# A hybrid attention and RWKV-7 layer: substitution of both token halves on 128 partitions, the correction systems as a second line of work, decay on the summed state, aligned tiles, other rates

## The chip, the core and the metric

The kernel runs on one core of a Trainium2 chip. The metric is device time in microseconds (us) of one execution; three executions were timed, and one more was profiled. In the profile PE is the matrix engine (PEld its weight loads), DVE the vector engine, ACT the scalar engine, POOL the GpSimd engine, SP the engine that issues most DMAs. SBUF is the on-chip memory of 128 partitions, PSUM the matmul's accumulators. L540 is line 540 of the kernel.

## What is computed

One layer over 1024 tokens of width 1024, in float32. Half of the width is eight attention heads, the other half eight heads of a recurrence that runs over the tokens in both directions.

```python
h = _rms_norm(x, ln1_g[layer])
proj = h @ w_in[layer]                       # 1024 x 3328
q, k, v = ...; u = proj[..., 3 * ATTN_WIDTH:]
attn = _dilated_window_attention(q, k, v, q_norm_g[layer], k_norm_g[layer])
rwkv = _rwkv7_bidirectional(u, ...)
x = x + jnp.concatenate([attn, rwkv], axis=-1) @ w_out[layer]
h = _rms_norm(x, ln2_g[layer])
x = x + jnp.square(jax.nn.relu(h @ w_up[layer])) @ w_down[layer]

# the recurrence, per head and direction, state is 64 x 64
def step(state, inp):
    r_t, w_t, k_t, v_t, kk_t, a_t = inp
    s_kk = jnp.einsum('bhvk,bhk->bhv', state, kk_t)
    state = (state * w_t[:, :, None, :]
             - s_kk[..., None] * (kk_t * a_t)[:, :, None, :]
             + v_t[..., None] * k_t[:, :, None, :])
    return state, jnp.einsum('bhvk,bhk->bhv', state, r_t)
```

Attention is a mixture of three dilated windows with normed queries and keys.

## The kernel before

**Matmuls.** Values and weights of the large products are split into a high and a low part (`split_w`, L101 on ACT and L102 on DVE), and `mm3` (L104 to L107) adds three products of 128x512. There are 1248 of them in the input projection, 384 in the output projection, 3072 in the MLP.

**Projection.** `dense` is a generator that makes one tile of 128 columns after the other, in the fixed list `order`, and yields after every six matmuls; a tile is 48 matmuls. Tiles of the recurrence are mixed with their neighbour tokens and stay in SBUF; q, k and v tiles are normed (`qk_tile`, the small PE products `psq`) or transposed and written to DRAM.

**Preparation of the recurrence.** The tokens are cut into 16 chunks of 64. For each of four head pairs p, two token halves hf (8 chunks each) and two directions d, `unit_a` makes what a chunk needs: decayed keys and values in `al` and `bk`, their products G (PE `psg` L501, masked by DVE L506), and the transposed keys `BK` (PE `psb` L517). Before the transposes POOL multiplies the keys by the chunk's whole decay into `bks` (L512). Most of it goes to the DRAM records `rec_dr`. Then 64x64 triangular systems are solved. Their 16x16 diagonal blocks are taken through DRAM (`gd`) into `MP`, 64 partitions holding the 64 blocks of 8 chunks and 2 heads, and are inverted by forward substitution: 15 steps, each a product on DVE (`stmp`, L540) and a sum (L542) into `Tt`, which two POOL memsets start. The result goes through the DRAM scratch `td` into `t16` and `t16t`. `unit_c` then completes the inverse by four groups of 16 small products (PE `psd`, L560), each followed by one DVE operation (L566, L572, L575). All tiles of a unit have one buffer, but for G, kt, t16t and Yt with two.

**Order of the work.** `merge` interleaves two yields of one unit's `unit_a` with one of the `unit_c` before it; `drive` runs that and gives `dense` 0.35 yields after each. What is left of the projection runs between the steps of the recurrence. The program is written in this order with priorities (`ahead`), and a scheduler then sets the order on each engine, which is fixed: an instruction that waits holds up what is behind it on its engine, and on SP every DMA behind it.

**Recurrence.** `mixers` runs 16 steps, in each one chunk forward and one backward (`step`). A step is three dependent groups of eight products in `psc` (L846, L854, L859) with copies between them. The state of the next chunk is the third group plus the old state times the chunk's decay LC; POOL makes that product (`pl`, L852), DVE adds (L861). `fill(20, 6)` puts 20 yields of projection, or once that is done 6 pieces of attention, behind each step. There are 64 pieces of attention, 8 for each head, and the ends of the four head pairs.

**Tail.** `tail` does the output projection with what is left of attention, the second norm and the MLP in four groups of an up phase and a down phase of 384 matmuls each.

The scheduling calls before the change are these:

```python
drive(per_half(w), rate)
for d in range(2):
    prev = drive(merge(unit_a(p * 4 + hf * 2 + d, w, d), prev), rate)
```

Of the kernel before, what the change touches and what calls it, by code (L numbers as in the profile page):

```python
# [16 lines left out]
P = 128  # L17
# [30 lines left out]
def tile_trunk(ctx: ExitStack, tc: tile.TileContext, xT, w_in, w_o, w_up, w_dn, vecs, w2w0, a2, g2, cst, att,  # L48
# [102 lines left out]
    qg8 = cp.tile([P, 1], F32, name="qg8")  # L151
    nc.vector.tensor_scalar(qg8, V("qg"), HD ** -0.5, None, ALU.mult)
# [9 lines left out]
    def in_proj():  # L162
        with ExitStack() as st:
# [36 lines left out]
            with tc.tile_pool(name="xp", bufs=2, side="right", reuse_waits="tile") as xp:  # L200
# [49 lines left out]
                rstd = hp.tile([P, 8], F32, name="rstd")  # L250
# [115 lines left out]

            def until(c):
# [15 lines left out]

            def merge(a, prev):
                c = unit_c(prev) if prev is not None else iter(())
                pat = 'aac'
                i = 0
                v = None
                while a is not None or c is not None:
                    which = pat[i % len(pat)] if i < 100 else 'a'  # L390
                    i += 1
                    if (which == 'a' or c is None) and a is not None:
                        try:
                            next(a)
                        except StopIteration as e:
                            v = e.value
                            a = None
                    else:
                        if next(c, 1) == 1:
                            c = None  # L400
                    yield
                return v
# [49 lines left out]
            def unit_a(u, w, d):  # L452
# [57 lines left out]
                bks = up.tile([P, 8, 2, 64], F32, name="bks")  # L510
                for h in range(2):
                    nc.gpsimd.tensor_mul(bks[H[h]], bk[H[h], :, h:h + 2],  # L512
                                         lc[H[h]].rearrange("p (c o x) -> p c o x", o=1, x=1).to_broadcast([64, 8, 2, 64]))
                pss = [pg.tile([P, 8, 64], F32, name="psb", tag="psg") for h in range(2)]
                for c in range(8):
                    for h in range(2):
                        nc.tensor.transpose(pss[h][:, c], bks[H[h], c].rearrange("p a b -> p (a b)"), K("id2")[H[h]])  # L517
                yield
                BK = up.tile([P, 8, 2, 64], F32, name="BK", tag="bks")
# [3 lines left out]
                MP = up.tile([64, 16, 16], F32, name="MP")  # L523
                nc.sync.dma_start(MP, diag(gd))
                Ab = up.tile([P, 8, 64], F32, name="Ab")
                for h in range(2):
                    nc.sync.dma_start(Ab[H[h]], mats(gd, h))
# [4 lines left out]
                Tt = up.tile([64, 16, 16], F32, name="Tt")  # L532
                Tp = up.tile([64, 16, 16], F32, name="Tp")
                nc.gpsimd.memset(Tt, 0.0)
                nc.gpsimd.memset(Tt.rearrange("p a b -> p (a b)")[:, 0:256:17], 1.0)  # L535
                for s in range(1, 16):
                    t = s if d == 0 else 15 - s
                    rs = slice(0, s) if d == 0 else slice(16 - s, 16)
                    tmp = up.tile([64, 16, 16], F32, name="stmp")
                    nc.vector.tensor_mul(tmp[:, 0:s, 0:s], Tt[:, rs, rs],  # L540
                                         MP[:, rs, t:t + 1].rearrange("p a o -> p o a").to_broadcast([64, s, s]))
                    nc.vector.tensor_reduce(Tt[:, rs, t], tmp[:, 0:s, 0:s], axis=AX.X, op=ALU.add)  # L542
                nc.vector.tensor_copy(Tp, Tt.rearrange("p a b -> p b a"))
                t16 = up.tile([P, 8, 64], F32, name="t16")
                t16t = up.tile([P, 8, 64], F32, name="t16t", bufs=2)
                for src, dst, td in ((Tp, t16, tdr[u % 2]), (Tt, t16t, tdr[2 + u % 2])):
                    nc.sync.dma_start(diag(td), src)
                    for h in range(2):
                        nc.sync.dma_start(dst[H[h]], mats(td, h))
                return dict(p=p, d=d, cs=cs, Ab=Ab, t16=t16, t16t=t16t)  # L550
# [47 lines left out]
            prev = None  # L598
            for p in range(4):
# [18 lines left out]
                rate = (0.35,0.35,0.35,0.35,0.35)[p]  # L618
                for hf in range(2):
                    w = dict(p=p, hf=hf, kr=kr, rr=rr, vr=vr, wh=wh, wl=wl, kt=[])  # L620
                    drive(per_half(w), rate)
                    for d in range(2):
                        prev = drive(merge(unit_a(p * 4 + hf * 2 + d, w, d), prev), rate)
                        if d == 1:
                            drive(bonus(w), rate)
            drive(unit_c(prev), (0.35,0.35,0.35,0.35,0.35)[4])
# [188 lines left out]
    def mixers(st, st2, filler, T, tqs, pq_):  # L815
# [24 lines left out]
        def step(d, s, w, wn, psY):  # L840
# [8 lines left out]
            if wn is not None:  # L849
                pl = rt.tile([P, 4, 64], F32, name=f"pl{d}")  # L850
                for h in range(2):
                    nc.gpsimd.tensor_mul(pl[H[h]], pv[H[h], :, H[h]], LC[H[h], d, c].rearrange("p (r o) -> p r o", o=1).to_broadcast([64, 4, 64]))  # L852
# [4 lines left out]
            if wn is not None:  # L857
                for r, h in RH:
                    nc.tensor.matmul(ps[H[h], 0, r], rec[:, r, 256 + h * 64:320 + h * 64], uv[:, r, H[h]], start=True, stop=True)  # L859
                for h in range(2):  # L860
                    nc.vector.tensor_add(wn["pv"][H[h], :, H[h]], ps[H[h], 0], pl[H[h]])  # L861
# [312 lines left out]
```

## Time and profile before

| | us |
|---|---|
| median of the timed executions | 1860.64 |
| lowest and highest of the three | 1854.66, 1874.15 |
| the profiled execution | 1866.15 |
| its span, first to last instruction | 1864.4 |
| mean granted clock of PE | 0.922 |

A row of a table of stretches gives, after the stretch and its length, the busy time of each engine with its number of instructions, the granted clock of PE as a share of full speed, the mean busy share of the 16 DMA engines, and GB/s. Overlapping matmuls count once. A row of a group gives line, engine, operation, written tile, read tiles, shape and count, then busy time and mean ns of one, then the idle time just before them and what ended it. A row of a source line gives the shortest, median and longest duration in ns. A row of the timeline gives start, duration, instruction and count. A row of waits gives who waited for whom, us in total, times, longest us.

### The profile page before, as it was taken

To read this page: it belongs to the slowest core of one execution; us is meant where nothing else is said; L and a number is where in the kernel's file an instruction comes from. 1 tells how busy PE (TensorE), PEld (TensorE's weight loads), DVE (VectorE), ACT (ScalarE), POOL (GpSimd) and SP (SyncE) were. 2 spreads that over 40 slices of the span, in tenths; PEclk is the share of its full clock that TensorE was granted. 3 is DMA by queue.
4 is the path that set the end of the run, shared out by engine and by line. 5 is a ranking of instruction groups with operands and counts; after the bars stand their busy time and mean duration, and the time that the engine had idled before them with its cause. 6 is when DMAs were issued, how large, how long until landed. Compare 5 with 4: busy or idle time off the path is not lost.

```text
span 1864.4 us, 30214 instructions
## 1 busy us (share of the span) xinstructions
PE 1718.9 (92%) x11912; PEld 1401.8 (75%) x11912; DVE 919.7 (49%) x1941; ACT 547.0 (29%) x994; POOL 365.5 (20%) x409
## 2 busy tenths in 40 slices
PE   7999988899866999899899869999999999999999
PEld 6776767677655788688788757888888888888887
DVE  6677868787864344256554437432233233223321
ACT  5533323443310232255452415211121112112210
POOL 3043234352340111112110015210121012001200
PEclk9998978788865999889879889999999999999999
DMA  6157675688785986999683211111111111111121
GB/s 201 36 130 163 146 150 119 143 181 188 151 165 122 291 255 183 195 238 264 186 237 78 78 44 57 45 46 51 51 46 46 46 50 47 51 46 46 46 91 57
DMA packets 336285, 222.06 MB, mean 119 GB/s; under 512 B 237936, under 2 KB 289024, under 8 KB 332048
## 3 DMA queue, kind: packets, MB, share of 16 engines
q1 hardware_dynamic: 305520, 195.82, 40.5%
q10 hardware_dynamic: 27040, 14.31, 2.8%
q0 software_dynamic: 3584, 10.00, 2.5%
q8 instruction: 94, 1.54, 0.4%
q14 instruction: 47, 0.39, 0.1%
HBM read 150.22 MB, written 69.84 MB: 118 GB/s over the span
## 4 chain that ended last, share of the span: by engine, by line
PE 47%; issue 1%; DMA 1%; DVE 1%; POOL 1%; ACT 1%; SPq 0%; ACTq 0%; DVEq 0%; POOLq 0%
PE ps L105 14%; PE ps L106 14%; PE ps L107 14%; PE pvb L729 1%; PE ps_s L684 1%; PE ps_s L685 1%; PE ps_pt L723 1%; PE pv L711 0%; PE pv L710 0%; PE ps_pt L702 0%; PE ps_t L798 0%; DMA w3raw<-in_w_o 0%; POOL sq L1026 0%; POOL on L794 0%; DVE y L886 0%
## 5 line engine op out<-in xcount | busy, mean ns | idle before, releaser
L101 ACT CAST w3h<-w3raw 128x512 fp32r<-128x512 f32 (+1 forms) x152 | 90.9, 598 | 391.3 <-PE ps L106 386.8
L106 PE MATMUL ps<-h2l,w3h 128*128 128x512 f32 x512 | 202.6, 396 | 0.6 <-DVE h2l L1019 0.6
L105 PE MATMUL ps<-h2h,w3h 128*128 128x512 f32 x512 | 202.4, 396 | 0.7 <-DVE x L997 0.7
L107 PE MATMUL ps<-h2h,w3l 128*128 128x512 f32 x512 | 202.5, 395 | 0.0
L1063 POOL TENSOR_TENSOR relu<-relu 128x512 f32<-128x512 f32 x64 | 76.7, 1200 | 543.1 <-DVE relu L1062 543.1
L105 PE MATMUL ps_u<-hh,wh 128*128 128x512 f32 x368 | 156.1, 424 | 2.8 <-DVE ur L305 2.3
L107 PE MATMUL ps_u<-hh,wl 128*128 128x512 f32 x368 | 155.1, 421 | 0.0
L106 PE MATMUL ps_u<-hl,wh 128*128 128x512 f32 x368 | 155.0, 421 | 0.0
L102 DVE TENSOR_TENSOR w3l<-w3raw,w3h 128x512 fp32r<-128x512 f32 (+1 forms) x152 | 106.7, 702 | 79.2 <-ACT w3h L101 79.1
L1071 DVE TENSOR_TENSOR x<-x,ps 128x512 f32<-128x512 f32 x64 | 44.0, 688 | 187.6 <-PE ps L107 187.6
L540 DVE TENSOR_TENSOR stmp<-Tt,MP 64x1 f32<-64x1 f32 (+14 forms) x240 | 105.4, 439 | 47.8 <-POOL Tt L535 28.7
L105 PE MATMUL ps<-f,w3h 128*128 128x512 f32 x320 | 126.6, 397 | 0.6 <-ACT f L806 0.6
L106 PE MATMUL ps<-rw,w3h 128*128 128x512 f32 x320 | 126.8, 396 | 0.0
L105 PE MATMUL ps<-rw,w3h 128*128 128x512 f32 x320 | 126.7, 397 | 0.0
L107 PE MATMUL ps<-rw,w3l 128*128 128x512 f32 x320 | 126.6, 396 | 0.0
L106 PE MATMUL ps<-f,w3h 128*128 128x512 f32 x320 | 126.6, 396 | 0.0
L107 PE MATMUL ps<-f,w3l 128*128 128x512 f32 x320 | 125.2, 392 | 0.0
L105 PEld LDWEIGHTS ps<-h2h,w3h 128*128 128x128 f32 x512 | 96.2, 188 | 24.6 <-ACT w3h L101 1.1
L106 PEld LDWEIGHTS ps<-h2l,w3h 128*128 128x128 f32 x512 | 96.2, 188 | 24.5 <-DVE h2l L1019 1.1
L107 PEld LDWEIGHTS ps<-h2h,w3l 128*128 128x128 f32 x512 | 96.3, 188 | 23.7
L1062 DVE SCALAR_TENSOR_TENSOR relu<-ps,rep 128x512 f32<-128x512 f32 x64 | 44.1, 691 | 116.4 <-PE ps L107 116.2
L105 PEld LDWEIGHTS ps_u<-hh,wh 128*128 128x128 f32 x368 | 73.5, 200 | 21.6 <-DVE ur L305 2.9
(324 smaller groups left out, 3410.7 us busy)
## 6 DMA issues: line engine op xcount, KB each, us to landing
rec<-rec_dr SPq DMA_DIRECT2D x32, 1152.0 KB, 8.9
w3raw<-in_w_up SPq DMA_DIRECT2D x64, 256.0 KB, 2.7
w3raw<-in_w_dn SPq DMA_DIRECT2D x64, 256.0 KB, 2.7
raw<-in_w_in SPq DMA_DIRECT2D x46, 256.0 KB, 3.2
rec_dr<-al POOLq DMA_DIRECT2D x64, 128.0 KB, 3.9
rec_dr<-G SPq DMA_DIRECT2D x32, 256.0 KB, 4.6
rec_dr<-G SPq DMA_DIRECT2D x64, 128.0 KB, 3.7
rec_dr<-BK ACTq DMA_DIRECT2D x16, 512.0 KB, 4.8
```

Source lines behind the costliest of these rows:

```text
L101: nc.scalar.copy(hi, raw)
L102: nc.vector.tensor_sub(lo, raw, r2f(hi))
L105: nc.tensor.matmul(ps, lh, rh, start=start, stop=False)
L106: nc.tensor.matmul(ps, lh, rl, start=False, stop=False)
L107: nc.tensor.matmul(ps, ll, rh, start=False, stop=stop)
L540: nc.vector.tensor_mul(tmp[:, 0:s, 0:s], Tt[:, rs, rs], MP[:, rs, t:t + 1].rearrange("p a o -> p o a").to_broadcast([64, s, s]))
L684: nc.tensor.matmul(ps[:, i], qh[:, qs], kk[:, ks], start=True, stop=False)
L685: nc.tensor.matmul(ps[:, i], ql[:, qs], kk[:, ks], start=False, stop=True)
L723: nc.tensor.transpose(pt[:, x, i * P:(i + 1) * P], sb[:, i, x * P:(x + 1) * P], ident)
L1062: nc.vector.scalar_tensor_tensor(t, pss[hf], 0.0, rep[:, HS[hf]], ALU.max, ALU.mult)
L1063: nc.gpsimd.tensor_mul(t, t, t)
L1071: nc.vector.tensor_add(x1[c][:, HS[hf]], x1[c][:, HS[hf]], ps)
```

## The change

1. `unit_a` ends with the writes to DRAM. A new generator `pair_b` takes both token halves of a head pair and direction: the half hf lies on its 64 partitions of `MP`, `Tt`, `Tp` and `stmp`, so 120 products and 120 sums of 128 partitions are issued instead of 240 and 240 of 64. There are eight pairs of `td` scratch instead of four.
2. `pair_b` then runs `unit_c` for one half and the other. These generators wait in the list `back`, which `behind` advances by 0.6 yields after each yield of the preparation and by 0.3 after each forced yield of the projection; `merge` is gone. What is left is run out at the end with four yields of projection after each of its own.
3. POOL's multiplies L512 and L852 are gone. The keys are transposed unscaled, and DVE multiplies the sum of products and old state by the decay.
4. `drive` gives 0.7 instead of 0.35 yields of projection, and `fill(20, 4.7)` 4.7 pieces of attention a step instead of 6.
5. The tile `rst` of 24 floats, and a tile `rest3` of 504 floats that nothing reads, shift those allocated after them. Before, in bytes past a multiple of 128, the projection's activations began at 32 and its weights at 64, the second norm's output `h2h` and `h2l` and the tiles `rw` at 32, the tiles `f` and the tail's weights at 96. After, all begin at multiples of 2048.

```diff
+    rst = cp.tile([P, 24], F32, name="rstd")
+    rstd = rst[:, 0:8]
...
-                for i in range(4):
+                for i in range(8):
                     td = dr.tile([64, 1040], F32, name=f"td{i}")
...
+            def behind(n):
+                due[0] += n
+                while due[0] >= 1.0:
+                    due[0] -= 1.0
+                    while back and next(back[0], 1) == 1:
+                        back.pop(0)
...
             def until(c):
                 while c not in T:
                     next(filler)
+                    behind(0.3)
...
             def drive(g, rate):
...
-                        with ahead(0):
-                            next(g)
+                        next(g)
                     except StopIteration as e:
                         return e.value
+                    behind(0.6)
...
-                bks = up.tile([P, 8, 2, 64], F32, name="bks")
-                for h in range(2):
-                    nc.gpsimd.tensor_mul(bks[H[h]], bk[H[h], :, h:h + 2],
-                                         lc[H[h]].rearrange("p (c o x) -> p c o x", o=1, x=1).to_broadcast([64, 8, 2, 64]))
...
+            def pair_b(q, p, d, gds):
+                MP = up.tile([P, 16, 16], F32, name="MP")
+                for hf in range(2):
+                    nc.sync.dma_start(MP[H[hf]], diag(gds[hf]))
...
                 for s in range(1, 16):
...
-                    tmp = up.tile([64, 16, 16], F32, name="stmp")
+                    tmp = up.tile([P, 16, 16], F32, name="stmp")
...
+                    if s in (5, 9, 12):
+                        yield
...
+                for hf in range(2):
+                    for src, td in zip((Tp, Tt), tds[hf]):
+                        nc.sync.dma_start(diag(td), src[H[hf]])
+                yield
+                for hf in range(2):
...
+                    yield from unit_c(dict(p=p, d=d, cs=slice(hf * 8, hf * 8 + 8), Ab=Ab, t16=t16, t16t=t16t))
...
-                    drive(per_half(w), rate)
+                    drive(per_half(w), 0.7)
                     for d in range(2):
-                        prev = drive(merge(unit_a(p * 4 + hf * 2 + d, w, d), prev), rate)
+                        gds[hf, d] = drive(unit_a(p * 4 + hf * 2 + d, w, d), 0.7)
+                        if hf == 1:
+                            back.append(pair_b(p * 2 + d, p, d, [gds[z, d] for z in range(2)]))
...
+            while back:
+                behind(1.0)
+                for _ in range(4):
+                    next(filler, None)
...
-            if wn is not None:
-                pl = rt.tile([P, 4, 64], F32, name=f"pl{d}")
-                for h in range(2):
-                    nc.gpsimd.tensor_mul(pl[H[h]], pv[H[h], :, H[h]], LC[H[h], d, c].rearrange("p (r o) -> p r o", o=1).to_broadcast([64, 4, 64]))
...
-                    nc.vector.tensor_add(wn["pv"][H[h], :, H[h]], ps[H[h], 0], pl[H[h]])
+                    new = wn["pv"][H[h], :, H[h]]
+                    nc.vector.tensor_add(new, ps[H[h], 0], pv[H[h], :, H[h]])
+                    nc.vector.tensor_mul(new, new, LC[H[h], d, c].rearrange("p (r o) -> p r o", o=1).to_broadcast([64, 4, 64]))
...
-            fill(20, 6)
+            fill(20, 4.7)
...
+            x1p.tile([P, 504], F32, name="rest3")
```

The order of the instructions moves at three places that the prediction speaks of. The first is PE at the end of the preparation. Before, from the last transposes of a unit (`psb`) to the first projection tile (`ps_u`), the products of the last three `unit_c` (`psd`) follow each other:

```order
L517 MATMUL psb<-ct,bks 128x64 x16
L560 MATMUL psd<-t_5043,Ab 64x64 x16
L560 MATMUL psd<-t16t,Nb 64x64 x16
L560 MATMUL psd<-Yt,Nb 64x64 x32
L560 MATMUL psd<-t_5418,Ab 64x64 x16
L560 MATMUL psd<-t16t,Nb 64x64 x16
L560 MATMUL psd<-Yt,Nb 64x64 x32
L560 MATMUL psd<-t_5706,Ab 64x64 x16
L560 MATMUL psd<-t16t,Nb 64x64 x16
L560 MATMUL psd<-Yt,Nb 64x64 x32
L342 MATMUL psq<-ct,vc 128x128 x4
L105 MATMUL ps_u<-hh_128,wh 128x512
```

Now two of them stand between the halves of projection tiles, of 24 `ps_u` matmuls each:

```order
L105 MATMUL ps_u<-hh_136,wh 128x512
L106 MATMUL ps_u<-hl_144,wh 128x512
L107 MATMUL ps_u<-hh_136,wl 128x512
L562 MATMUL psd<-Yt,Nb 64x64 x16
L124 MATMUL psq<-ct,qsq 128x2 x4
L562 MATMUL psd<-t_5123,Ab 64x64 x16
L136 MATMUL psq<-ct,rx 128x128 x4
L105 MATMUL ps_u<-hh_129,wh 128x512
```

From the last `psb` of the preparation to the first product of the recurrence PE's order holds 20 projection matmuls before and 210 now; over all of PE's order ahead of that product there are 908 and 1080. Behind it 340 and 168 are left, and 325 of the 792 matmuls of attention stand ahead of the last product of the recurrence before, 709 now.

The second is DVE in the first steps of the recurrence, where `pv` is the state and `psc` the products. Before, with the product `pl` from POOL:

```order
L861 TENSOR_TENSOR pv_5866<-psc_5881,pl_5892 64x4x64 x2
L856 COPY uv_5857<-psc_5931 64x4x64
L861 TENSOR_TENSOR pv_5874<-psc_5931,pl_5942 64x4x64 x2
L856 COPY uv_5869<-psc_6273 64x4x64
L127 TENSOR_SCALAR rn<-psq 128x8
L128 RECIPROCAL rn<-rn 128x8
L102 TENSOR_TENSOR wl<-raw,wh 128x512
```

Now, with two multiplies by LC more behind each pair of sums:

```order
L864 TENSOR_TENSOR pv_6372<-psc_6387,pv_6352 64x4x64 x2
L865 TENSOR_TENSOR pv_6372<-pv_6372,LC 64x4x64 x2
L858 COPY uv_6363<-psc_6436 64x4x64
L858 COPY uv_6375<-psc_6675 64x4x64
L127 TENSOR_SCALAR rn<-psq 128x8
L128 RECIPROCAL rn<-rn 128x8
L864 TENSOR_TENSOR pv_6380<-psc_6436,pv_6360 64x4x64 x2
L865 TENSOR_TENSOR pv_6380<-pv_6380,LC 64x4x64 x2
```

The third is SP's queue in the preparation, at the write-out of a substitution (`td`). Before, a unit's two write-outs and the loads back stand ahead of the next G writes:

```order
L547 DMA td_362<-Tt 64x16x16
L547 DMA td_356<-Tp 64x16x16
L549 DMA t16t<-td_362 64x8x64
L549 DMA t_2797<-td_356 64x8x64 x2
L549 DMA t16t<-td_362 64x8x64
L509 DMA gd_3288<-G 64x8x64
L529 DMA rec_dr_84<-G 64x8x128
```

Now a pair's four write-outs stand together, and the loads of its first half come before the next G writes:

```order
L541 DMA td_369<-Tp 64x16x16
L541 DMA td_372<-Tt 64x16x16
L541 DMA td_375<-Tp 64x16x16
L541 DMA td_378<-Tt 64x16x16
L590 DMA bon_dr<-us 128x512
L522 DMA MP<-gd_1754 64x16x16
L548 DMA Ab<-gd_842 64x8x64 x2
L196 DMA raw<-in_w_in 128x512
L551 DMA t_1941<-td_369 64x8x64 x2
L551 DMA t16t<-td_372 64x8x64 x2
L502 DMA gd_1971<-G 64x8x64 x2
```

More of the change, by code (lines that the diff above doesn't have):

```diff
@@ L365, in in_proj @@
             credit = [0.0]
+            back = []
+            due = [0.0]
+            def behind(n):
[4 more added lines that the diff above has]
+                        back.pop(0)
             def until(c):
@@ L382, in drive @@
                         next(filler, None)
[L384 to L402, printed above, removed]
             def gates():
@@ L516, in unit_a @@
                     for h in range(2):
-                        nc.tensor.transpose(pss[h][:, c], bks[H[h], c].rearrange("p a b -> p (a b)"), K("id2")[H[h]])
+                        nc.tensor.transpose(pss[h][:, c], bk[H[h], c, h:h + 2].rearrange("p a b -> p (a b)"), K("id2")[H[h]])
                 yield
-                BK = up.tile([P, 8, 2, 64], F32, name="BK", tag="bks")
+                BK = up.tile([P, 8, 2, 64], F32, name="BK")
                 for h in range(2):
@@ L538, in unit_a @@
                     rs = slice(0, s) if d == 0 else slice(16 - s, 16)
-                    tmp = up.tile([64, 16, 16], F32, name="stmp")
+                    tmp = up.tile([P, 16, 16], F32, name="stmp")
                     nc.vector.tensor_mul(tmp[:, 0:s, 0:s], Tt[:, rs, rs],
-                                         MP[:, rs, t:t + 1].rearrange("p a o -> p o a").to_broadcast([64, s, s]))
+                                         MP[:, rs, t:t + 1].rearrange("p a o -> p o a").to_broadcast([P, s, s]))
                     nc.vector.tensor_reduce(Tt[:, rs, t], tmp[:, 0:s, 0:s], axis=AX.X, op=ALU.add)
+                    if s in (5, 9, 12):
+                        yield
                 nc.vector.tensor_copy(Tp, Tt.rearrange("p a b -> p b a"))
[L544 to L547, printed above, removed]
-                    for h in range(2):
-                        nc.sync.dma_start(dst[H[h]], mats(td, h))
-                return dict(p=p, d=d, cs=cs, Ab=Ab, t16=t16, t16t=t16t)
+                tds = [[tdr[q % 2 * 4 + hf * 2 + i] for i in range(2)] for hf in range(2)]
+                for hf in range(2):
+                    for src, td in zip((Tp, Tt), tds[hf]):
+                        nc.sync.dma_start(diag(td), src[H[hf]])
+                yield
+                for hf in range(2):
+                    Ab = up.tile([P, 8, 64], F32, name="Ab")
+                    t16 = up.tile([P, 8, 64], F32, name="t16")
+                    t16t = up.tile([P, 8, 64], F32, name="t16t", bufs=2)
+                    for h in range(2):
+                        nc.sync.dma_start(Ab[H[h]], mats(gds[hf], h))
+                    for dst, td in zip((t16, t16t), tds[hf]):
+                        for h in range(2):
+                            nc.sync.dma_start(dst[H[h]], mats(td, h))
+                    yield from unit_c(dict(p=p, d=d, cs=slice(hf * 8, hf * 8 + 8), Ab=Ab, t16=t16, t16t=t16t))
             def unit_c(v):
@@ L597, in in_proj @@
             until(8)
-            prev = None
             for p in range(4):
@@ L848, in step @@
             nc.scalar.copy(B, ps[:, 0])
-            if wn is not None:
-                pl = rt.tile([P, 4, 64], F32, name=f"pl{d}")
-                for h in range(2):
-                    nc.gpsimd.tensor_mul(pl[H[h]], pv[H[h], :, H[h]], LC[H[h], d, c].rearrange("p (r o) -> p r o", o=1).to_broadcast([64, 4, 64]))
             for r, h in RH:
```

17 lines of the change are left out of this document (6 added, 11 removed).

## The prediction

> **What bounds the kernel now.** I first read the busy times, then one table of engine work over seven stretches cut where the work changes: start, preparation of the recurrence with projection tiles between its pieces, end of that preparation, the recurrence in two parts (with projection tiles, then with attention), output projection with the rest of the attention, MLP.
>
> ```profile
> PE 1718.9 (92%) x11912; PEld 1401.8 (75%) x11912; DVE 919.7 (49%) x1941; ACT 547.0 (29%) x994; POOL 365.5 (20%) x409
> ```
> ```profile
> core 0: us, PE busy (x) PEld busy (x) DVE busy (x) ACT busy (x) POOL busy (x), PEclk, DMA share, GB/s
> 0.00:97.00 97.00, 83.10 (x363) 66.28 (x364) 61.61 (x79) 50.02 (x62) 18.01 (x34) 0.98 0.36 115
> 97.00:551.00 454.00, 397.72 (x3458) 313.14 (x3457) 354.25 (x764) 156.03 (x246) 169.53 (x203) 0.86 0.71 153
> 551.00:603.00 52.00, 32.32 (x412) 28.34 (x412) 23.78 (x65) 1.21 (x2) 4.13 (x11) 0.53 0.57 127
> 603.00:764.00 161.00, 156.28 (x1824) 128.14 (x1825) 58.48 (x123) 47.30 (x104) 22.05 (x37) 0.98 0.83 234
> 764.00:920.00 156.00, 137.23 (x1734) 117.54 (x1731) 82.11 (x273) 76.93 (x175) 28.02 (x34) 0.88 0.91 232
> 920.00:1155.00 235.00, 206.60 (x1091) 178.74 (x1091) 126.31 (x323) 99.81 (x221) 47.02 (x27) 0.87 0.37 106
> 1155.00:1864.00 709.00, 705.66 (x3045) 569.56 (x3044) 213.15 (x317) 115.67 (x187) 76.73 (x64) 1.00 0.16 51
> ```
> PE is the busiest engine in every stretch, but its clock is not whole: where it idles between pieces it is granted less. I call busy time times granted clock the PE work of a stretch: 81, 342, 17, 153, 121, 180 and 706 us. Over time that is 84%, 75%, 33%, 95%, 78%, 77% and 100%. So the MLP can only get shorter by faster matmuls, while about 260 us are lost to gaps and half clock before it. DVE, busy for 354 of 454 us, is what PE shares the second stretch with. The third stretch is a bare chain:
>
> ```profile
> 586.67 1.97 PE L560 MATMUL psd<-t16t,Nb 64*64 64x64 f32 x32 [0.78 <-DVE Nb L566]
> 589.44 1.97 PE L560 MATMUL psd<-Yt,Nb 64*64 64x64 f32 x32 [0.79 <-DVE Yt L572]
> 592.20 1.97 PE L560 MATMUL psd<-Yt,Nb 64*64 64x64 f32 x32 [0.79 <-DVE Yt L572]
> ```
> One product of 16 matmuls each 2.76 us, 0.79 of it waiting for DVE, the rest at half clock (1.97 us; 0.98 at full).
>
> **Preparation, 97 to 551.** Two parts of the change relieve DVE here.
>
> ```profile
> L540 DVE TENSOR_TENSOR stmp<-Tt,MP x240: 103/290/3459, 127.4 to 575.2; 64x1 f32<-64x1 f32 x8, 64x9 f32<-64x9 f32 x8, 64x25 f32<-64x25 f32 x8, 64x49 f32<-64x49 f32 x8
> ```
> ```profile
> L540 DVE TENSOR_TENSOR stmp<-Tt,MP 64x1 f32<-64x1 f32 (+14 forms) x240 | 105.4, 439 | 47.8 <-POOL Tt L535 28.7 <-DMA MP<-gd 13.7
> L512 POOL TENSOR_TENSOR bks<-bk,EE 64x1024 f32<-64x1024 f32 x32 | 64.0, 1999 | 54.9 <-DMA rec_dr<-BK 36.2 <-DVE Nb L566 9.4 <-PE psg L501 8.0
> L542 DVE TENSOR_REDUCE Tt<-stmp 64x1 f32<-64x1 f32 (+14 forms) x240 | 55.1, 229 | 5.9
> ```
> ```profile
> 351.71 3.46 DVE L540 TENSOR_TENSOR stmp<-Tt,MP 64x196 f32<-64x196 f32 x1
> ...
> 352.90 4.06 POOL L512 TENSOR_TENSOR bks<-bk,EE 64x1024 f32<-64x1024 f32 x2
> ```
> The substitution costs 105.4 + 55.1 = 160.5 us in 480 instructions of 64 partitions. One of them took 3.46 us and ended near the end of POOL's two scaling multiplies, so DVE was held while POOL read. The mean product is 439 ns against a median of 290: 240 x 0.149 = 36 us of hold (bounds: 0, or all 64 us of those multiplies). The scaling goes, so I take 36. Of the other 124 us half goes, since twice the partitions go through at the same row lengths.
>
> ```profile
> 97.00:551.00 454.00, 97.98 (x217) 0.86 0.71 153
> ```
> 217 of the 240 products, 14.5 of 16 units, lie in this stretch today; of the change's 8 pairs about six and a half do, so 124 x (14.5/16) - 62 x (6.5/8) = 62 us leave it. DVE falls from 354 to about 257.
>
> PE work hardly changes: in the new order 870 projection matmuls instead of 888 stand before the last transposes of the preparation (-18 x 0.233 = -4), and 96 fewer of the correction products (-6): 332 us. DVE is then no longer near PE's load, and gaps, with the clock they cost, shrink. Bounds: today's 75% (443 us), or the 95% that the stretch after it reaches with the same matmuls (350). I take 84%, nearer the middle, because the units still follow each other through single buffers: 396, so **-58**.
>
> **Its end, 551 to 603.** The products of the last units now have projection matmuls between them: 210 matmuls (49 us), 288 for products (18 x 0.98 = 18) and 64 small ones of the norms at 0.14 (9): 76 us, at 95% 80. The chain beneath, 18 x 2.76 = 50, is covered; without cover it would be added. **+28**, work brought forward.
>
> ```profile
> 335.50 1.11 PE L136 MATMUL psq<-ct,rx 128*128 128x128 f32 x4
> ```
>
> **Recurrence, 603 to 920.** From 153 + 121 = 274 us of PE work leave 172 projection matmuls (40) and 77 small ones (11); 384 attention matmuls come in. Their price: in the stretch from 920, 432 matmuls of 128x512 take 432 x 0.233 = 101 of 180 us,
>
> ```profile
> 920.00:1155.00 235.00, 110.28 (x432) 0.87 0.37 106
> ```
> (a table of the tail's matmuls alone), so 79 are left for 467 attention matmuls and a few others: 0.16 each, 61 us. Together 284. A step costs about (153 - 340 x 0.233 - 117 x 0.14)/8 = 7 us without them. The 168 projection matmuls that stay (39), with their norms (6) and three and a half steps (25), run at 95%: 74. The other 214 run as the attention part does today, at 78%: 274. Sum 348, **+31**. Bounds: 70% gives 380, 90% gives 312.
>
> ```profile
> L852 POOL TENSOR_TENSOR pl<-pv,LC x60: 605/612/1114, 595.0 to 889.0; 64x256 f32<-64x256 f32 x60
> L861 DVE TENSOR_TENSOR pv<-psc,pl x60: 365/423/429, 614.0 to 907.7; 64x256 f32<-64x256 f32 x60
> ```
> Here the decay moves from POOL (60 x 0.61 = 37 us, beside other work) onto DVE behind the sum: 60 multiplies of about 0.42, two more on each direction's chain, 0.85 a step. Hidden, because a pair of steps takes about 20 us (317/16) and the other direction and attention run meanwhile; DVE would be busy about 60%. Queued behind them on DVE are attention's score reductions and projection outputs. If all of it showed: 30 x 0.85 = 25 us.
>
> **Output projection, 920 to 1155.** 180 - 61 = 119 us of work. Today 55 us are lost, largely to attention's chain; with 83 instead of 467 matmuls of it left I take 33: 152, **-83** (bounds: 130 and 174).
>
> Eight more zero-fills of scratch go out on ACT's queue at the start, 8 x 0.37 = 3 us of issue (next row), covered because the scratch is needed only by the first pair.
>
> ```profile
> 335.66 0.37 ACTq L522 DMA_DIRECT2D rec_dr<-BK  x1
> ```
>
> **Aligned tiles.** The padding adds no instruction; it moves the projection's and the tail's matmul operands from 32 or 96 bytes past a multiple of 128 to multiples of 2048. The trace has no such operand in a 512-column matmul, only two unaligned cases (12 and 21 starts on):
>
> ```profile
> 1262.04 0.39 PE L105 MATMUL ps<-rw,w3h 128*128 128x512 f32 x1
> ...
> 1264.84 0.39 PE L105 MATMUL ps<-f,w3h 128*128 128x512 f32 x1
> ```
> ```profile
> 1123.36 0.39 PE L106 MATMUL ps<-f,w3h 128*128 128x512 f32 x1
> ...
> 1128.12 0.39 PE L106 MATMUL ps<-f,w3h 128*128 128x512 f32 x1
> ```
> ```profile
> 1237.10:1325.80 88.70, 88.70 (x386) 71.97 (x385) 11.01 (x16) 1.00 0.16 48
> 1325.80:1415.40 89.60, 89.60 (x386) 71.81 (x385) 11.05 (x16) 1.00 0.15 48
> ```
> ```profile
> 337.26 0.63 PE L107 MATMUL ps_u<-hh,wl 128*128 128x512 f32 x1
> ...
> 339.82 0.63 PE L107 MATMUL ps_u<-hh,wl 128*128 128x512 f32 x1
> ```
> Starts are 2.80/12 = 0.233 us apart where moving operand (rw, 32 past) and weights (96 past) differ in place, and 4.76/21 = 0.227 where both (f) lie 96 past. At half clock six starts take 2.56: 0.427, or 0.2135 at full clock, the floor. Today's 384 matmuls of an up phase take 89.6 (0.2333), those of a down phase 88.7 (0.231). After the change operand and weights again lie alike, so the nearest row is 0.227: 1536 x 0.0063 + 1920 x 0.004 = 17 us in tail and output projection, 1104 x 0.006 = 7 in the projection: **-24**. Bounds: 0, and the floor: 1536 x 0.0198 + 1920 x 0.0175 + 1104 x 0.0195 = 86.
>
> The Trainium skill, "TensorE: Matmul & The Clock Gate", section "Wait — 56ns, not 53.3ns?", has 215.7 ns between 512-column matmuls at full clock; by it the term would be an estimated 75. The measured 227 and 233 are above it, and no run here shows it. Against any gain speaks "SBUF — State Buffer" of the Trainium skill, section on the DMA port swizzle: lines of SBUF are 16 bytes, so a start 32 bytes off would already be whole. That both rows above start on whole 16-byte lines and still differ by 6 ns does not fit it.
>
> **Sum.** -58 + 28 + 31 - 83 - 24 = -106, from the profiled execution's 1866.15 us: 1760. The runs' median, 1860.64, lies 5.5 below that execution, so I predict **1755 us**.
>
> **Rivals.** (a) Alignment gives nothing, since no aligned operand stands in the trace to show that it does: 1755 + 24 = 1779. Against it are the two rows above. The 16-byte lines of the Trainium skill's "SBUF — State Buffer" lead here. (b) Alignment reaches the floor or nearly: 24 less, 75 to 86 more gone, 1693 to 1704, say 1698. For it, the half-clock rows keep exactly to the column count; against it, no full-clock row does. (c) Filling does not do what it should: the preparation keeps its 454 us because the single-buffered unit chain sets the pace, not DVE, and the denser attention runs at 70%: +58 + 32 = 1845, no change. For it, PE is busy 398 of 454 us already; against it, the granted clock of 0.86 there says those gaps come from waiting, and DVE was the partner. (d) The slower case is one mechanism: SP's queue.
>
> ```profile
> SPq L576 <- DVE stmp L540: 16.4, 5, 12.9
> SPq L547 <- DVE Tt L542: 17.2, 3, 9.9
> SPq L509 <- DVE stmp L540: 17.3, 7, 6.4
> ```
> SP already stands up to 9.9 us at the write-out of a finished substitution. That substitution is now cut into portions behind other work, four write-outs and the loads waiting for them stand in SP's order before the next units' writes of G, and G's two buffers hold up the units. A hold of 9.9 us on each of 16 units gives 1755 + 158 = 1913; it decides from about 6.6 us a unit. Against it: today the three rows add up to 51 us, most of them covered.
>
> **Chances.** My forecast 0.45, (a) 0.20, (b) 0.20, (c) 0.10, (d) 0.05. About 1% is what a measurement of this kernel can tell from no change. All but (c) and (d) are faster by more; of (c) I count 0.03 as faster and 0.07 as within 1%; (d) is slower, with 0.01 from beyond the list: faster 0.87, same 0.07, slower 0.06. The range holds (a), (b) and the spread of the stage terms (+-46 in the preparation, +-35 in the recurrence, +-22 after it, not all one way): 1690 to 1825.
>
> **What would show it.** Right: first recurrence matmul near 573 instead of 603 with a granted clock above 0.9 over the preparation; no POOL scaling and no stmp instruction of several us; last recurrence matmul near 920 with attention nearly done; MLP start some 80 us earlier; starts of 128x512 matmuls 0.227 apart, the same in up and down phases. Wrong: a preparation as long as today with SP or single buffers named as what is waited for; a recurrence beyond 380 us; up phases still at 89.6 (a) or near 83 (b).

## The result and the profile after

The changed kernel takes 1801.07 us (median of four runs, 1799.31 to 1803.82) against 1858.4 for the kernel before on the same chip. The ratio is 0.9677, 95% interval 0.9619 to 0.9735: 57 us faster by the medians and 60 by the ratio, where I had forecast 105. The profiled execution has a span of 1799.0 us, against 1864.4. A run more than 1.5% above the fastest of its kernel counts as slow and is left out; of all the runs below that is one, of run 7, at 1855.80 us.

Busy times of the whole span, then engine work by stretches of the changed kernel. The stretches are cut at the last transposes of the preparation (526), the first and last matmul of the recurrence (625.7 and 972.0) and the first matmul of the MLP's up projection (1093.6). Columns as in the table of the kernel before.

```profile
PE 1688.9 (94%) x11912; PEld 1391.0 (77%) x11912; DVE 851.4 (47%) x1753; ACT 554.3 (31%) x998; POOL 249.2 (14%) x301
```
```profile
97.00:526.00 429.00, 381.13 (x3302) 301.57 (x3302) 261.60 (x532) 164.08 (x256) 95.62 (x156) 0.86 0.76 162
526.00:625.70 99.70, 84.76 (x870) 70.00 (x864) 48.19 (x106) 21.20 (x35) 1.60 (x6) 0.94 0.56 144
625.70:972.00 346.30, 324.96 (x3755) 277.78 (x3757) 180.84 (x565) 150.31 (x364) 20.64 (x18) 0.93 0.84 223
972.00:1093.60 121.60, 115.10 (x535) 95.43 (x535) 75.63 (x147) 46.91 (x88) 27.03 (x18) 0.92 0.32 106
1093.60:1799.00 705.40, 700.56 (x3104) 580.00 (x3104) 223.86 (x328) 122.38 (x197) 86.73 (x70) 1.00 0.16 52
```
The kernel before, cut at the same events from its recurrence on:

```profile
603.40:918.70 315.30, 291.81 (x3540) 244.06 (x3539) 139.84 (x394) 122.94 (x274) 50.07 (x70) 0.93 0.87 233
918.70:1140.50 221.80, 194.63 (x1037) 169.60 (x1038) 112.67 (x314) 93.46 (x214) 33.15 (x20) 0.86 0.38 109
1140.50:1864.40 723.90, 718.93 (x3104) 579.94 (x3104) 227.55 (x328) 123.31 (x197) 90.60 (x72) 1.00 0.16 51
```
Read from the end. The tail is 18.5 us shorter with all its 3104 matmuls. The stretch ahead of it fell from 221.8 to 121.6 us, since most of attention now lies in the recurrence, which grew from 315.3 to 346.3. Then comes the surprise: the recurrence begins **later**, at 625.7 instead of 603.4, although DVE is busy 261.60 us in the preparation instead of 354.25. That 179 more projection matmuls (787 against 608 from 97 us on) now stand ahead of it, some 41 us at 0.227 each, was in my forecast of 573; that the stretches would still be long was not. PE's granted clock in the preparation is still 0.86.

| stretch | predicted us | measured us |
|---|---|---|
| preparation, 97 to the last transposes | 396 | 429.0 |
| its end, to the first recurrence matmul | 80 | 99.7 |
| recurrence | 348 | 346.3 |
| from there to the end (152 + 709, less 17 of the aligned tiles) | 844 | 827.0 |

The 7 us of the aligned tiles in the projection are not taken off the forecasts of the first rows.

What PE waited for in the preparation, after and before (us in total, times, longest us):

```profile
PE psg L494 <- DVE G L499: 13.4, 7, 5.0
PE psd L562 <- DVE Nb L568: 8.5, 1, 8.5
PE pse L452 <- ACT om L441: 7.6, 3, 3.2
PE psg L494 <- DVE al L473: 3.4, 1, 3.4
```
```profile
PE psg L501 <- DVE G L506: 17.9, 10, 3.5
PE psd L560 <- DVE Yt L572: 10.0, 5, 4.3
PE psd L560 <- DVE Nb L566: 5.5, 2, 4.4
PE psg L501 <- POOL al L479: 3.5, 2, 2.3
```
The waits for Yt, in the chain of products, are no longer among the longest. Those for G, the masked copies that free the units' PSUM, are still the largest; one wait of 8.5 us for Nb and waits for ACT (om) have come. I look at G first, in DVE's instructions and SP's queue around 250 us of the changed kernel (start, duration):

```profile
246.95 0.69 DVE L499 TENSOR_TENSOR G<-psg,ct 128x512 f32<-128x512 f32 x1 [0.65 <-DMA rec_dr<-G]
251.94 0.69 DVE L499 TENSOR_TENSOR G<-psg,ct 128x512 f32<-128x512 f32 x1 [4.30 <-DMA rec_dr<-G]
```
```profile
246.30 1.98 SPq L578 DMA_DIRECT2D rec_dr<-TF  x1
248.33 1.18 SPq L515 DMA_DIRECT2D rec_dr<-G  x1
```
```profile
252.69 2.07 PE L494 MATMUL psg<-al,bk 64*128 64x128 f32 x14 [2.98 <-DVE G L499]
```
The last write of the unit before from G's buffer goes out at 248.33, behind another write in SP's order; DVE's copy has to wait for it until 251.94, and PE 2.98 us for the copy. DVE itself stands idle for 4.30 us before that copy, so it is not DVE's load that PE meets here. The Nb wait is of the same kind:

```profile
404.63 0.16 DVE L532 TENSOR_TENSOR stmp<-Tt,MP 128x1 f32<-128x1 f32 x1 [7.76 <-DMA MP<-gd]
...
406.11 0.68 DVE L568 TENSOR_TENSOR Nb<-psd,ct 128x512 f32<-128x512 f32 x1
```
DVE stands 7.76 us for the blocks of the next pair, and Nb, whose products PE had started at 393.57, stands behind in DVE's order. And gaps of this size can be paid a second time. The same place in short windows (the column after POOL is the granted clock):

```profile
244.80:251.60 6.80, 4.91 (x87) 4.09 (x82) 1.39 (x2) 1.27 (x1) 0.00 (x0) 1.00 0.99 213
251.60:258.50 6.90, 5.81 (x51) 5.15 (x53) 3.57 (x7) 2.09 (x5) 0.44 (x2) 0.51 0.87 164
258.50:265.30 6.80, 5.01 (x70) 3.67 (x66) 1.80 (x3) 1.61 (x3) 0.00 (x0) 1.00 1.17 203
265.30:272.10 6.80, 5.39 (x43) 4.35 (x43) 1.99 (x3) 3.60 (x6) 1.04 (x1) 0.50 1.02 231
272.10:275.50 3.40, 1.81 (x35) 1.19 (x33) 0.02 (x1) 1.11 (x3) 0.05 (x1) 1.00 0.43 95
275.50:296.00 20.50, 19.54 (x130) 16.10 (x131) 16.98 (x22) 7.67 (x11) 10.21 (x17) 0.50 0.61 124
```
Windows with 1.6 to 1.9 us of idle PE (6.80 - 4.91, 6.80 - 5.01, 3.40 - 1.81) are each followed by one at half clock, the last of them 20.5 us long though PE is nearly always busy in it. Fifteen stretches at half clock, 123 of the 429 us, make the mean clock of 0.86 of the preparation; before it was 128 of 454 us, so this loss hardly changed.

In the end of the preparation, where I had forecast 80 us, 99.7 - 84.76 x 0.94 = 20 us are lost. The largest single piece is the last: PE waits for the load of `pv` from `vt_dr`.

```profile
PE psc L852 <- DMA pv<-vt_dr: 6.0, 1, 6.0
```

### The profile page after: what moved, and what is told of

Same layout as the page of the kernel before. It is cut to its first block, busy times and chain, and to the rows that moved or that the text cites. A ratio compares the mean times of both kernels' runs of the same rounds, so it can differ in the third digit from the quotient of the medians.

```text
span 1799.0 us, 29847 instructions
## 1 busy us (share of the span) xinstructions
PE 1688.9 (94%) x11912; PEld 1391.0 (77%) x11912; DVE 851.4 (47%) x1753; ACT 554.3 (31%) x998; POOL 249.2 (14%) x301
## 5 line engine op out<-in xcount | busy, mean ns | idle before, releaser
L105 PE MATMUL ps<-f,w3h 128*128 128x512 f32 x320 | 124.7, 390 | 0.0
L106 PE MATMUL ps<-f,w3h 128*128 128x512 f32 x320 | 124.5, 389 | 0.0
L106 PEld LDWEIGHTS ps_u<-hl,wh 128*128 128x128 f32 x368 | 74.5, 202 | 17.5 <-issue 2.7
```

The lines of the kernel that those rows point to most:

```text
L105: nc.tensor.matmul(ps, lh, rh, start=start, stop=False)
L106: nc.tensor.matmul(ps, lh, rl, start=False, stop=False)
```

## The experiments

Each run is compared by its ratio to the kernel before on its own chip; the changed kernel's is 0.9677, known to +-0.0058 or 11 us. For the length of the preparation I use the units' stretch, from 97 us to the last product of the units (psg), and call what is not PE work there (length less busy time times granted clock) its loss. Its rows for the two kernels and the four runs that changed one engine's load:

```profile
97.00:540.20 443.20, 393.65 (x3409) 309.87 (x3409) 346.76 (x741) 154.95 (x244) 168.69 (x201) 0.87 0.72 155
```
```profile
97.00:518.60 421.60, 373.73 (x3224) 296.08 (x3222) 254.81 (x509) 162.96 (x253) 95.62 (x156) 0.86 0.75 161
```
These are before and after: 443.20 - 393.65 x 0.87 = 101 us lost, and 421.60 - 373.73 x 0.86 = 100, with DVE 92 us lighter.

**1. Aligned tiles undone in the changed kernel.**

```
-    rst = cp.tile([P, 24], F32, name="rstd")
-    rstd = rst[:, 0:8]
+                rstd = hp.tile([P, 8], F32, name="rstd")
...
-            x1p.tile([P, 504], F32, name="rest3")
...
-                rstd = rst[:, 8:16]
+                rstd = hp.tile([P, 8], F32, name="rstd3")
```


> The changed kernel with its tiles put back where they were (32 or 96 bytes past a multiple of 128). Theory: the place of the tiles alone moves the start-to-start time of 128x512 matmuls, 226.7 ns in the tail of the changed kernel against 233.4 (h2h, rw) and 228.4 (f) before. Then 1536 x 6.7 + 960 x 6.6 + 960 x 1.7 ns = 18 us come back in the tail and about 4 in the projection: 1801 + 22 = 1823. Rival: the shorter spacing comes from something else in the new order, and this kernel takes 1801 with 226.7 ns.

1820.29 us, ratio 0.9796 (0.9744 to 0.9848): 19 us by the medians, 22 by the ratios. Matmuls of the tail in the same place, changed kernel and this one:

```profile
1189.72 0.39 PE L107 MATMUL ps<-rw,w3l 128*128 128x512 f32 x1
...
1192.89 0.39 PE L106 MATMUL ps<-f,w3h 128*128 128x512 f32 x1
```
```profile
1189.74 0.39 PE L107 MATMUL ps<-h2h,w3l 128*128 128x512 f32 x1
...
1192.77 0.40 PE L105 MATMUL ps<-h2h,w3h 128*128 128x512 f32 x1
```
14 starts in 3.17 us, 0.226 each, against 13 in 3.03, 0.233 each. The units' last product (519.9) and the first recurrence matmul (627.2) stay where they were. So the place of the tiles alone makes the term.

**2. What of the place counts: all tiles together 32 bytes on.**

```
-    rst = cp.tile([P, 24], F32, name="rstd")
+    rst = cp.tile([P, 32], F32, name="rstd")
...
-            x1p.tile([P, 504], F32, name="rest3")
+            x1p.tile([P, 496], F32, name="rest3")
```


> The changed kernel with all tiles of the projection and the tail moved by 32 bytes together, so that moving operand and weights again begin alike but 32 past a multiple of 128. Theory (what counts is that both begin alike): 226.7 ns in the tail and 1801 us as in the changed kernel. Rival (what counts is a begin at a multiple of 128 or 64): 233 ns for all tiles, f too, and 1801 + 22 to 26.

1795.22 us, ratio 0.9706 (0.9669 to 0.9744), as the changed kernel within the error.

```profile
1189.66 0.39 PE L107 MATMUL ps<-rw,w3l 128*128 128x512 f32 x1
...
1192.83 0.39 PE L106 MATMUL ps<-f,w3h 128*128 128x512 f32 x1
```
Again 14 starts in 3.17 us. The rival falls: a begin at a multiple of 128 is not needed, only that moving operand and weights begin alike. This holds for the places tried, both 0 and both 32 past; slow were 32 against 64 and 32 against 96.

**3. The decay alone, in the kernel before.**

```
-                bks = up.tile([P, 8, 2, 64], F32, name="bks")
...
-                pl = rt.tile([P, 4, 64], F32, name=f"pl{d}")
...
-                    nc.vector.tensor_add(wn["pv"][H[h], :, H[h]], ps[H[h], 0], pl[H[h]])
+                    new = wn["pv"][H[h], :, H[h]]
+                    nc.vector.tensor_add(new, ps[H[h], 0], pv[H[h], :, H[h]])
+                    nc.vector.tensor_mul(new, new, LC[H[h], d, c].rearrange("p (r o) -> p r o", o=1).to_broadcast([64, 4, 64]))
```


> The kernel before with one part of the change: no scaled copy on POOL, the decay on DVE after the sum. Theory A (the chain of single-buffered steps sets the pace of the preparation, DVE's load does not): the 36 us of hold on DVE turn into little, at most 10 us, 1848 to 1858. Theory B (DVE is the partner, as the prediction had it): 36 us of hold are 36 us of preparation, 1822. If the decay on DVE showed in the recurrence, up to 25 us would be added to either, seen there.

1853.91 us (ten runs), ratio 0.9982 (0.9953 to 1.0011): -2 us, between -9 and +2.

```profile
97.00:521.20 424.20, 389.34 (x3313) 305.01 (x3312) 303.53 (x714) 156.24 (x244) 104.02 (x167) 0.87 0.74 159
```
DVE is 43 us lighter in the units' stretch, about the 36 priced; the 240 products take 76.9 us instead of 105.4. In this one execution (1848.80 us, the second fastest of its ten) the units end 19 us earlier and the recurrence begins 9 us earlier; in the median almost nothing is left. Theory B falls for this part. The recurrence itself is 351.1 us long instead of 315.3, with the same 340 projection matmuls, but 168 instead of 116 score products of attention (`ps_s`) lie in it, and the stretch behind it is 181.5 us instead of 221.8. The two together are 4 us shorter, so a cost of 25 us for the decay does not show; the length of the recurrence alone does not tell.

**4 and 5. The substitution in the changed kernel: on 64 partitions again, and left out.**

```
-                    nc.vector.tensor_reduce(Tt[:, rs, t], tmp[:, 0:s, 0:s], axis=AX.X, op=ALU.add)
+                    for hf in range(2):
...
+                        nc.vector.tensor_reduce(Tt[H[hf], rs, t], tmp[H[hf], 0:s, 0:s], axis=AX.X, op=ALU.add)
```


> The changed kernel, the substitution again on 64 partitions: each instruction in two, one for each half, so that DVE has 240 instead of 120 products and sums and some 67 us more to do, nearly all before 626 us. Theory A (chain): DVE has room, at most 10 us more, 1801 to 1811. Theory B (DVE): half of it or more shows, 1835 to 1868.

```
-                    nc.vector.tensor_mul(tmp[:, 0:s, 0:s], Tt[:, rs, rs],
...
-                    nc.vector.tensor_reduce(Tt[:, rs, t], tmp[:, 0:s, 0:s], axis=AX.X, op=ALU.add)
```


> The changed kernel without the products and sums of the substitution (the inverse of the diagonal blocks stays the identity): DVE loses the 67 us that remain. Theory A (chain): the first recurrence matmul stays within 10 us of 626 and the time at 1791 to 1801. Theory B (DVE): half of it or more is gained, 1734 to 1768.

On 64 partitions: 1826.59 us, ratio 0.9837 (0.9789 to 0.9885), 25 to 30 us more. Left out: 1788.04 us, ratio 0.9647 (0.9579 to 0.9714), 13 us less by the medians and 6 by the ratios. Rows of the units' stretch, in this order:

```profile
97.00:547.60 450.60, 400.40 (x3280) 318.66 (x3279) 313.73 (x703) 161.13 (x254) 95.68 (x156) 0.85 0.70 154
```
```profile
97.00:522.30 425.30, 390.44 (x3387) 309.56 (x3385) 220.15 (x331) 160.44 (x252) 94.55 (x156) 0.89 0.75 162
```
The first lies between the theories: DVE is busy 66 us more over the whole span (917.1 instead of 851.4), and about 0.4 of that shows. The second lies between them too, near theory A: DVE is busy 56 us less (795.3), and 0.1 to 0.2 of that shows. The units end at 522.3, no earlier than with the substitution. But the first recurrence matmul comes at 603.3, 22 us earlier, where theory A had it within 10 us of 626; 24 fewer projection matmuls ahead of it (763 against 787) are some 5 of these 22. The order of PE's instructions differs a little in these kernels (fewer or more projection matmuls fall into the units), so single stretches are rougher than the totals.

**6. The substitution left out of the kernel before**, the same products and sums (the loop over its steps is empty).

> The kernel before without the products and sums of the substitution: DVE loses 160 us of work, 145 of it in the preparation, and the units lose that step. Theory A (of what DVE loses 0.2 to 0.37 shows, as in the two runs that changed the substitution): 1799 to 1826. Theory B (0.52 and more shows, as the prediction priced it): 1775 or less.

1803.1 us, ratio 0.9705 (0.9656 to 0.9755): 55 to 57 us, 0.35 of the 160 priced for DVE and 0.42 of the 132 by which its busy time fell (919.7 to 787.5). Theory A, by the time.

```profile
97.00:512.60 415.60, 386.98 (x3511) 302.37 (x3509) 237.46 (x330) 156.16 (x245) 160.00 (x199) 0.90 0.79 167
```
With DVE at 237.46 us this kernel loses 67 us; the changed one, at 254.81, loses 100. So DVE's load alone does not set the loss. With the substitution left out of both the losses are 78 and 67, and the changed kernel is only 0.0058 of the time, 11 us, faster, less than the aligned tiles alone are worth. That the new order of the work gained time by itself is not shown; the new handovers (a result passed from one engine to the next) may have cost some.

**7. More load on SP: the six writes of G twice a unit, the second time to a scratch table.**

```
+    gx_dr = [dr.tile([P, NCH, 4, RW], F32, name=f"gx_dr{d}") for d in range(2)]
...
+                    nc.sync.dma_start(gx_dr[d][H[1 - h], cs, p, h * P:h * P + P], Gs[h][H[1 - h]])
+                    nc.sync.dma_start(gx_dr[d][H[h], cs, p, h * P + 64:h * P + P], Gs[h][H[h], :, 64:128])
+                    nc.sync.dma_start(gx_dr[d][H[1 - h], cs, p, 448 + h * 64:512 + h * 64], Gs[h][H[1 - h], :, 64:128])
```


> The changed kernel with the six writes of G to the recurrence's table issued twice a unit, the second time to a scratch table: 96 more transfers on SP, at 1.2 us of issue each 113 us more in the units' stretch. Theory S (SP's order and the transfers hold the units): most of it shows, 1840 to 1910. Rival (SP has room): 1801 to 1811. Between them the rise says which share of SP's issue time the units feel.

1829.60 us (three runs), ratio 0.9867 (0.9844 to 0.989): 29 to 35 us of 113, about 0.3 of it. Neither theory; the share is about that of DVE's load. The edit loads the DMA engines too (0.86 busy instead of 0.75), so the share of SP's issue time alone is at most this.

```profile
97.00:560.50 463.50, 400.37 (x3377) 317.27 (x3376) 261.97 (x516) 161.27 (x255) 92.86 (x156) 0.87 0.86 183
```
**8 to 10. Three attempts to take away one wait of the changed kernel.** G's writes on ACT's queue; two more turns between the load of a pair's blocks and its first product; a third buffer for G.

```
-                    nc.sync.dma_start(rec_dr[d][H[1 - h], cs, p, h * P:h * P + P], Gs[h][H[1 - h]])
+                    nc.scalar.dma_start(rec_dr[d][H[1 - h], cs, p, h * P:h * P + P], Gs[h][H[1 - h]])
...
```


> The changed kernel with the three write-outs of G to the recurrence's table issued on ACT's queue instead of SP's. Theory G (G has one set of buffers, and a unit's masked copy of its products waits until the unit before has written them out behind other transfers in SP's order: DVE stood 17.7 us for these writes and PE 15.9 us for G in the preparation): 16 us of gaps and about as much half clock go, 1770 to 1786. Rival (the transfers themselves are the limit, or another wait takes the place): at most 5 us, 1796 to 1803.

```
                 nc.gpsimd.memset(Tt.rearrange("p a b -> p (a b)")[:, 0:256:17], 1.0)
                 yield
+                yield
+                yield
```


> The changed kernel with two more turns between the load of a pair's diagonal blocks and its first product. Theory (DVE meets a product whose operand is still under way, 21.5 us in three waits, and the copies that PE waits for stand behind it in DVE's order, 8.5 us once): that wait and the half clock after it go, 1781 to 1793. Rival (the gap moves to the next single buffer): 1797 to 1803.

```
-                Gs = [up.tile([P, 8, P], F32, name="G", bufs=2) for h in range(2)]
+                Gs = [up.tile([P, 8, P], F32, name="G", bufs=3) for h in range(2)]
...
-                    wl = wp.tile([P, 4, P], F32R, name="wl", bufs=4)
+                    wl = wp.tile([P, 4, P], F32R, name="wl", bufs=3)
...
+                Tp = up.tile([P, 16, 16], F32, name="Tp", tag="stmp")
```


> The changed kernel with a third buffer for G, so that a unit's first masked copy needs no write-out of the unit before; the room comes from a fourth buffer of the projection's low weights and from the transposed substitution, which shares its scratch. Theory G (waits for G's buffers set the pace of the units): DVE's 17.7 us for these writes and most of PE's 15.9 us for G go, and half clock with them, 1775 to 1788. Rival (another wait of the units' chain takes their place): 1796 to 1806, with the units' last product near 519 as now.

1833.15 us (ratio 0.9875, 0.9818 to 0.9932), 1806.99 (0.9732, 0.9676 to 0.9789) and 1811.66 (0.9789, 0.9754 to 0.9825): none is faster, the first is slower by 32 to 37 us, and the third by 11 to 21, beyond the error by the ratios. In the first the load only changes its engine. The 96 issues of G's writes take 111.7 us of ACT's time, as they took 113.4 of SP's, and what stands behind them on ACT waits: from 181.56 to 188.16 us, for example, ACT does nothing else while four of them go out. Waits of ACT and PE in its preparation:

```profile
ACT BK L510 <- DMA rec_dr<-G: 25.7, 3, 11.5
...
PE psg L494 <- ACT bk L480: 18.1, 5, 5.7
```
PE now waits for ACT's copies (bk) instead of for G. With a third buffer DVE's wait for the writes halves, from 17.7 to 9.0 us (its two rows, changed kernel and this one):

```profile
  DMA rec_dr<-G: 17.7, 5
```
```profile
  DMA rec_dr<-G: 9.0, 2
```
and PE waits elsewhere: 8.9 us for G, but 8.2 for Yt and 6.7 for ACT's squares of the queries. The units' last product comes at 543.3, not near 519 as the rival had it. Theory G falls in the form in which I tried it, with one buffer less for the projection's low weights and 41 more projection matmuls in the units' stretch (612); which of these made it slower is open. The two turns more did not do what they were for: DVE's wait for the blocks, in the changed kernel and in that one, is

```profile
  DMA MP<-gd: 21.5, 3
```
```profile
  DMA MP<-gd: 30.8, 5
```
so what this wait costs stays untested.

**11. Projection steps at half the rate.** `drive(..., 0.7)` back to `drive(..., 0.35)`.

> The changed kernel with projection steps given at 0.35 a turn as before; the rest comes out at the end of the preparation, so that about the same number stands ahead of the recurrence. Theory A (the units' own chain sets the pace, and more filling does not slow it): units end no earlier, and what is moved to the end is added, 1815 to 1850. Rival (filling stands ahead of the units' matmuls in PE's order and delays them): units end earlier by about what is moved, 1795 to 1806.

1808.48 us, ratio 0.9716 (0.9656 to 0.9776): 7 us more, within the error. Neither theory is confirmed, because the edit did not thin out the filling: 606 projection matmuls lie in the units' stretch (it ends at 523.1) where the changed kernel has 571. The units call for most projection tiles themselves before they go on, so the rate decides little.

**12. The halves of queries and keys and the values written from ACT, which makes them.**

```
-                    nc.sync.dma_start((qh_dr, kh_dr)[which][p][:, sl], r2f(hi))
+                    nc.scalar.dma_start((qh_dr, kh_dr)[which][p][:, sl], r2f(hi))
...
-                        nc.sync.dma_start(v_dr[p][h, sl].rearrange("(t p) f -> p t f", p=P), vn[:, :, h])
+                        nc.scalar.dma_start(v_dr[p][h, sl].rearrange("(t p) f -> p t f", p=P), vn[:, :, h])
```


> The changed kernel with the write-outs of the high halves of queries and keys and of the values issued on ACT's queue, right behind the ACT copies that make them. SP loses 24 transfers and the 26 us that it stood waiting for these copies; ACT gets 24 issues of about 0.4 us and no wait for another engine. Theory (the units' chain feels 0.27 of what SP is relieved of, as in the run that doubled the writes of G): 26 us of waiting and 18 us of issue give 8 to 14 us, 1787 to 1793. Rival (no one queue sets the pace and another wait takes the place): 1797 to 1806.

1796.2 us (six runs), ratio 0.9658 (0.9628 to 0.9688): between the two expectations, and not to be told from the changed kernel. SP's wait for the high halves, 22.2 us, is gone, but its wait for the low ones, now first in its order, rose from 1.6 to 19.4.

## Why the prediction was right and where it failed

- **Aligned tiles, -24:** right in size, 19 to 22 us (runs 1 and 2). The tail's part of it, 17 with the output projection, measured 18 for the MLP alone. The floor (rival b) and nothing (rival a) are out. The reason I gave, that operand and weights lie alike, is what run 2 shows. The tail's matmuls start 0.2267 us apart, the 0.227 that I took.
- **Recurrence, +31:** right, 315.3 to 346.3, and with 168 projection matmuls left in it, where I had 168. No cost of the decay on DVE shows (run 3).
- **Output projection, -83:** 221.8 to 121.6 by the same events, 100. I had left 33 us of loss there; 121.6 - 115.10 x 0.92 = 16 are left. These 17 us too many offset a part of the next miss, which is luck.
- **Preparation and its end, -58 + 28 = -30:** wrong, +22. These 52 us are more than the whole miss, of which the output projection took 17 back. What I said of the work was right: DVE 262 us where I had 257, PE work 381.13 x 0.86 + 84.76 x 0.94 = 407 us where I had 408. The step that failed is "DVE is then no longer near PE's load, and gaps, with the clock they cost, shrink": I took 84% and 95%, and PE had 76% and 80%. The loss was 454 - 342 + 52 - 17 = 147 us before, 429 - 328 + 99.7 - 80 = 121 after, and 68 in the prediction. Of the 20 us lost in the end, 6.0 are one wait for the load of `pv`, a term that my 80 us did not have.
- **Its price:** of the 97 us that I took off DVE I let 48 show (58 less 10 of PE work), one half. Runs 3 to 6 put a microsecond of DVE at 0 to 0.4, run 7 one of SP at no more than about 0.3. So neither DVE's load nor SP's alone sets the pace. My reading is that a unit goes from PE to ACT to DVE to SP and back through buffers of one or two, that each handover costs its part, and that many gaps are paid again in half clock. The waits at 250 and 404 us are examples; no run shows it as a whole, since runs 8 to 10 shortened no time. What the second line of work added (a product that waits for its load with PE's copies behind it in DVE's order, 8.5 us once) may have taken back part of what it freed.
- **The 36 us of POOL hold:** they leave DVE, and the time changes by -9 to +2 us. At least three quarters of them bought nothing.
- **Rival (c)** was nearer for what holds the preparation (429 us, between its 454 and my 396) and wrong for attention, whose 70% did not come: PE has 324.96 x 0.93 / 346.3 = 87% in the recurrence. **Rival (d)** has its place, the writes of G in SP's order, as the rows at 250 us show, but not its price.

By parts, as far as the runs tell them apart: alignment 19 to 22, substitution on 128 partitions 25 to 30, decay 2 to 3. The remaining 5 to 11 of the 57 to 60 us are for the second line of work and the denser projection together. This is a difference of numbers that are each known to some 14 us, so it can't be told from nothing, and the placement was not tried alone. Open is which handover holds the units at some 26 us each, (518.6 - 105) / 16 from the first product to the last: the waits that I did shorten came back at other engines.

## What to carry to other kernels

When several engines pass small pieces round through single buffers, expect a microsecond off one of them to give only a part of itself (here 0 to 0.4), not what its share of busy time suggests; ask which instruction PE stands at, and what that one waits for, before pricing the load. Count the larger gaps and not only their sum, since many bring a stretch at half clock. Place the moving operand and the weights of long matmul series at the same offset past a multiple of 128 bytes.

## What the runs showed of the hardware

- 128x512 matmuls start 0.226 to 0.227 us apart where both operands begin 0 or both 32 bytes past a multiple of 128, and 0.233 where they begin 32 against 64 or 32 against 96. The 215.7 ns of the Trainium skill, "TensorE: Matmul & The Clock Gate", section "Wait — 56ns, not 53.3ns?", did not come with either place.
- 1.6 to 1.9 us of idle PE in the three windows above, of 3.4 or 6.8 us, were followed by half clock; it then lasted 6.8 to 20.5 us, with PE busy 79% to 95% of the time. Not every such gap did this. Cut into slices of 3.41 us from 101 to 620 us, where the clock changes only from slice to slice, the changed kernel has 12 slices at full clock with 1.4 us or more of idle PE, and 11 of them are followed by half clock; in the kernel before it is 10 of 13. The way back is stricter. In the windows from 251.6 and 265.3 the idle 1.1 and 1.4 us lie in the first half, and PE is busy throughout the second, after which the full clock came back. Of the slices at half clock with 0.15 us or more of idle PE, 14 in the changed kernel and 28 before, none was followed by full clock. The Trainium skill, "TensorE: Matmul & The Clock Gate", section "HAM oscillation — how this bites in real kernels", names gaps over some 3.4 us as what to avoid; here a gap of 2.98 us was followed by half clock.
- Issuing a transfer takes the issuing engine's time: the 96 writes of G took 113.4 us on SP, 1.18 each, and 111.7 us on ACT, where ACT's own work stood behind them. Moving them to ACT cost 32 to 37 us.
